# Stick-breaking weights by a running product on VectorE, with TensorE's side work in the second layer in a written order

## The chip, the cores and the metric

The kernel runs on one core of a Trainium2 chip. The metric is the device time of one execution in microseconds, lower is better. A core has five engines that run their own instruction streams in order and wait for each other by semaphores: TensorE (PE; its weight loads are shown apart as PEld), VectorE (DVE), ScalarE (ACT), GpSimd (POOL) and SyncE (SP), which here issues the DMAs.

## The reference, cut to what matters

One inference step of a decoder of two layers, for 256 prompt rows and 8 sample rows (264 columns in the kernel's layout) at model width 1024. Layer 0 mixes tokens by block-sparse softmax attention and a gated mixer, layer 1 by stick-breaking attention (8 heads of 64) and a causal pooling mixer with windows 2, 4, 8, 16. Each is followed by a convolutional FFN of width 2816. Norms, projections and residual adds stand around them. What changes is the stick-breaking attention:

```python
z = einsum('bqhd,bkhd->bhqk', q, k) * scale
before = kpos[None, :] < pos[:, None]
log_keep = where(before, log_sigmoid(-z), 0.0)
later = cumsum(log_keep, axis=3, reverse=True) - log_keep
w = where(before, exp(log_sigmoid(z) + later), 0.0)
out = einsum('bhqk,bkhd->bqhd', w, v)
```

The weight of key s for query t is sigmoid(z_ts) times the product of 1 - sigmoid(z_tj) over all keys j between s and t. The 256 prompt rows see each other; each sample row sees 256 cached keys, which lie in pages found through a page table.

## The kernel before

Activations lie transposed, features on the 128 partitions and 264 token columns in the free dimension. All weights stream from memory in the order of use, in blocks of 128x128. `run` walks through the blocks of a phase. For each it issues three matmuls (lines 329 to 331), since weights and activations are split into a high and a low half in fp32r: high by high, high by low, low by high. The split of a tile of eight blocks is one copy on ScalarE (`wh`, line 306) and one subtraction on VectorE (`wl`, line 307), three tiles ahead. The phases per layer are input projection (`in0`, `in1`), output projection (`out0`, `out1`), FFN gate and up (`ff`), and FFN down (`dn`). In layer 1 the input projection has 128 blocks: q and k (four tiles of eight blocks each, the four q tiles interleaved by half), then u (for the pooling), then v; the output projection has 64.

Everything else is side work hung into `run` at block counts, through `Hooks`: `hk.at(n, f)` calls f once 8(n+1) blocks are through. In which order an engine's instructions then stand is set by the framework's planner, which lays the program out by its own cost estimate; instructions wrapped in `keep_in_program_order` stay in the order in which they are written. Matmuls of the projections are not wrapped before the change, most side products neither. PSUM has two pools of four banks: `psm` ("mm") for the projections, `psa` ("at") for side work. 24 SBUF buffers of one size (`up`) are shared by activations, cache pages and work tiles.

Side work of the second layer, before the change:

- `nrm1.finish()`: squares of the residual rows are added on GpSimd (line 398) while the first layer's `dn` ends; a matmul with ones (`ns_n`, line 406) sums them over the partitions; Ln and Exp on ScalarE make the factor `R`, with which VectorE scales each projection result as it leaves PSUM (`in1_evac`).
- `zs_score`, `zs_soft`, `zs_cum`: scores of the samples against the cached keys (`sc`, line 451, 64 matmuls), turned over with the identity (line 921), softplus, sums over the keys by matmuls with a triangle of -1 (`negU`, lines 928 and 929), Exp.
- `z_qk(t)`, for a pair of heads: a matmul of identity by mask (line 882) sets the forbidden places to -1e30, then scores with keys on the partitions and queries in the free dimension (lines 884, 886); softplus by three ScalarE passes (Abs, Exp, Ln) and one VectorE operation (line 876).
- `z_cum(h)`, per head: the softplus is split into two fp32r halves (`Lh` on ScalarE, `Ll` on VectorE, lines 413, 414), matmuls with `negU` and with -1 (lines 900, 901) add for each key the sum over the later keys onto the scores in PSUM, and one Exp (line 902) gives the weights, keys on the partitions, as the value product needs them.
- `z_av(t)` (`av`, lines 494, 495): weights times values for a pair of heads; `sample_av` (line 465) and `sample_out` (line 478) the same for the samples. `v_pair` (line 489) transposes a tile of v.
- `pool_sum(t, o)`: per u tile about ten VectorE operations (lines 947 to 964), and `pool_mix(t)` a matmul (line 969).

The first layer's softmax attention (`s_qk`, `s_soft`, `s_tr`) has scores with queries on the partitions, and turns its weights over with three transposes per head (`pt`, line 684).

Of the kernel before, what the change touches and what calls it, by code (L numbers as in the profile page):

```python
# [18 lines left out]
P = 128  # L19
# [42 lines left out]
VL = 9  # L62
SQ = 4
SMO = -0.5
VL1 = 4
SQ1 = 4.5
ZQ0 = 5
ZQ1 = 1
ZC = 1
PM = 13  # L70
ZSS = 4.75
ZSC = 6
ZSA = 13
ZSO = 14.75
NA = 4
NB_ = 0.5
NEG = -1e30
# [143 lines left out]
@with_exitstack  # L221
def tile_decoder_step(ctx: ExitStack, tc: tile.TileContext, a):
    nc = tc.nc
    v, s, g, pe = nc.vector, nc.scalar, nc.gpsimd, nc.tensor
# [85 lines left out]
    def run(order, rhs, evac, hooks=None):  # L310
# [5 lines left out]
        for m, k in order:  # L316
# [15 lines left out]
            if left[m] == 0:  # L332
                evac(m, o)
            n += 1
            while hooks and n >= 8 * (hooks[0][0] + 1):
                for f in hooks.pop(0)[1]:
                    f()

# [23 lines left out]
    ident = cst("ident")  # L362
    ones = con.tile([P, P], F32, name="ones")
    v.memset(ones, 1.0)
    nones = con.tile([P, P], F32, name="nones")
    v.memset(nones, -1.0)
    epst = con.tile([P, 1], F32, name="epst")
    v.memset(epst, EPS)

# [113 lines left out]
    PZ = con.tile([P, NPG, NS, 32], F32, name="PZ")  # L483
    g.memset(PZ, 0.0)

    def v_pair(vt, src, t, name):
        p = at(f"vtp_{name}{t}")
        for kb in range(2):
            pe.transpose(p[:, kb * P:(kb + 1) * P], src[:, kb * P:(kb + 1) * P], ident)
        s.activation(vt[:, :, t * P:(t + 1) * P], p[:, :2 * P].rearrange("p (b d) -> p b d", b=2), AF.Copy)  # L490
# [5 lines left out]

    def gelu_set():
        tc.keep_in_program_order(s.preload_act_table_set("gelu_apprx_tanh_and_others"))

    def lnexp():  # L500
        tc.keep_in_program_order(s.preload_act_table_set("natural_log_exp_and_others"))
# [112 lines left out]
    maskb1 = con.tile([P, 384], BF16, name="maskb1")  # L614
    identb = con.tile([P, P], BF16, name="identb")

    def masks():
        tc.keep_in_program_order(v.tensor_copy(maskb0[:, 0:P], cst("m0")))
        v.tensor_copy(maskb0[:, SEQ:384], cst("m0"))
        v.tensor_copy(maskb1[:, 0:P], cst("m1"))  # L620
        v.tensor_copy(maskb1[:, SEQ:384], cst("m1"))
        for mk in (maskb0, maskb1):
            g.memset(mk[:, P:SEQ], 0.0)
        v.tensor_copy(identb, ident)

    q4, k4, v4 = f4("q4"), f4("k4"), f4("v4")
# [237 lines left out]
    icnt = cst("icnt").rearrange("p (g i) -> p g i", g=4)  # L864
    st1 = {}

    negU = con.tile([P, P], F32R, name="negU")
    v.tensor_copy(negU, cst("negU"))
    nonesr = con.tile([P, P], F32R, name="nonesr")
    v.tensor_copy(nonesr, nones)  # L870

    def softplus(e, z):
        s.activation(e, z, AF.Abs)
        s.activation(e, e, AF.Exp, scale=-1.0)
        s.activation(e, e, AF.Ln, bias=1.0)
        v.scalar_tensor_tensor(e, z, 0.0, e, ALU.max, ALU.add)

    def z_qk(t):
        pss = [at(f"Z1_{2 * t + i}") for i in range(2)]
        hd = [(q4[b:b + 64, t, :], k4[b:b + 64, t, :]) for b in (0, 64)]  # L880
        for ps in pss:
            pe.matmul(ps[:, :384], identb, maskb1, start=True, stop=False, skip_group_check=True)
        for ps, (qh, kh) in zip(pss, hd):
            tc.keep_in_program_order(pe.matmul(ps[:, 0:SEQ], kh[:, 0:P], qh[:, 0:SEQ], start=False, stop=False, skip_group_check=True))  # L884
        for ps, (qh, kh) in zip(pss, hd):
            tc.keep_in_program_order(pe.matmul(ps[:, SEQ:384], kh[:, P:SEQ], qh[:, P:SEQ], start=False, stop=False, skip_group_check=True))
        for i, ps in enumerate(pss):
            L = pp.tile([P, 384], F32, tag="p", name=f"L1_{2 * t + i}")
            softplus(L, ps[:, :384])
            st1["z", 2 * t + i] = (ps, L)  # L890

    def z_cum(h):
        ps, L = st1.pop(("z", h))
        if h % 2 == 0:
            st1["w", h // 2] = f4(f"w1_{h // 2}", (P, 2, 384))
        lh = pp.tile([P, 384], F32R, tag="ph", name=f"Lh_{h}", bufs=2)
        ll = pp.tile([P, 384], F32R, tag="pl", name=f"Ll_{h}", bufs=2)
        halves(lh, ll, L)
        for x in (lh, ll):
            pe.matmul(ps[:, 0:384], negU, x, start=False, stop=False, skip_group_check=True)  # L900
            pe.matmul(ps[:, P:SEQ], nonesr, x[:, SEQ:384], start=False, stop=x is ll, skip_group_check=True)
        s.activation(st1["w", h // 2][:, h % 2, :], ps[:, :384], AF.Exp)

    def z_av(t):
        w = st1.pop(("w", t))
        pav = at(f"pav1_{t}")
        for hh in range(2):
            av(pav, vt, w[:, hh, :], 2 * t + hh)
        halves(catA[0][:, t, :SEQ], catA[1][:, t, :SEQ], pav[:, :SEQ])

    def zs_score():
        ps = at("sc1")
        sample_score(ps, sample_q(q4, "l1"), ktiles, range(NS))
        z = st1["zs"] = pp.tile([P, PAST], F32, tag="p", name="zs")
        s.activation(z, ps[:, :PAST], AF.Copy)

    def zs_soft():
        z = st1["zs"]
        pc = at("pc")
        for pg in range(NPG):  # L920
            pe.matmul(pc[:, pg * P:(pg + 1) * P], z[:, pg * P:(pg + 1) * P], ident, start=pg == 0, stop=False, skip_group_check=True)
        L = pp.tile([P, PAST], F32, tag="p", name="L1s")
        softplus(L, pc[:, :PAST])
        st1["Ls"] = pc, L

    def zs_cum():
        pc, L = st1["Ls"]
        pe.matmul(pc[:, :PAST], cst("negU"), L, start=False, stop=False, skip_group_check=True)
        pe.matmul(pc[:, :P], nones, L[:, P:PAST], start=False, stop=True, skip_group_check=True)
        to_pz(pc, AF.Exp)  # L930
        st1["msk"] = f4("msk1", (P, 2, 512))

    def zs_out():
# [31 lines left out]
        st1["pl", t] = pl  # L965

    def pool_mix(t):
        pm = at(f"pm{t}")
        pe.matmul(pm[:, :T], pw[:, t, :], st1.pop(("pl", t)), start=True, stop=True)
        hh, ll = catB[0][:, t, :], catB[1][:, t, :]  # L970
        gs = vec("ps")[:, t:t + 1]
# [3 lines left out]
    def in1_evac(m, o):  # L975
# [11 lines left out]
    hk.at(SQ1, zs_score)  # L987
    for t in range(4):
        hk.at(ZQ0 + 2 * ZQ1 * t, z_qk, t)
        for h in (2 * t, 2 * t + 1):  # L990
            hk.at(ZQ0 + ZQ1 * h + ZC, z_cum, h)
    hk.at(8, lambda: nc.sync.dma_start(a["k1"], k4))
    for t in range(4):
        hk.at(PM - t, pool_mix, t)
    for t in range(3):
        hk.at(13 + t, lambda t=t: v_pair(vt, v4[:, t, :], t, "v1"))
    hk.at(14, z_av, 0)
    hk.at(15, z_av, 1)
    hk.at(15, z_av, 2)
    hk.at(ZSS, zs_soft)  # L1000
    hk.at(ZSC, zs_cum)
    hk.at(ZSA, sample_av_of(st1, PZ, vtiles, 0, "l1"))
    hk.at(ZSA + 1, sample_av_of(st1, PZ, vtiles, 1, "l1"))
    hk.at(ZSO, zs_out)
# [12 lines left out]
    _, nrm, evac = residual(vec("fin"), "fin", operand=False)  # L1017
# [71 lines left out]
```

## Time and profile before

| | us |
|---|---|
| runs: median of 3 (lowest to highest) | 618.79 (618.44 to 619.36) |
| profiled execution | 618.47 |
| its span | 616.4 |
| TensorE busy, share of the span | 97% |
| VectorE busy, share of the span | 67% |
| ScalarE busy, share of the span | 57% |

Granted TensorE clock over the span: 0.996 of full speed. The span runs from the first to the last instruction; about 2 us of an execution lie around it. Matmuls are pipelined, so the length of one (about 0.28 us) is more than its distance to the next (about 0.12); what one costs TensorE is read from starts. A start in the timeline is in microseconds from the span's start, followed by the length, and in brackets the engine's idle time before it and what ended that. In the rows by group, the numbers behind the bar are busy us, mean ns of one instruction, and idle time before. A window's row has its length, and then busy time and number of instructions of PE, PEld, DVE, ACT and POOL, the granted clock, the DMA share, and GB/s. In the chain of waits a row is start, length, and the work.

### The profile page before, as it was taken

To read this page: it belongs to the slowest core of one execution; us is meant where nothing else is said; L and a number is where in the kernel's file an instruction comes from. 1 tells how busy PE (TensorE), PEld (TensorE's weight loads), DVE (VectorE), ACT (ScalarE), POOL (GpSimd) and SP (SyncE) were. 2 spreads that over 40 slices of the span, in tenths; PEclk is the share of its full clock that TensorE was granted. 3 is DMA by queue.
4 is the path that set the end of the run, shared out by engine and by line. 5 is a ranking of instruction groups with operands and counts; after the bars stand their busy time and mean duration, and the time that the engine had idled before them with its cause. 6 is when DMAs were issued, how large, how long until landed. Compare 5 with 4: busy or idle time off the path is not lost.

```text
span 616.4 us, 12351 instructions
## 1 busy us (share of the span) xinstructions
PE 599.4 (97%) x4924; PEld 575.3 (93%) x4924; DVE 413.1 (67%) x704; ACT 350.4 (57%) x621; POOL 84.9 (14%) x111
## 2 busy tenths in 40 slices
PE   7899999999999999999999999999999999999994
PEld 5788987999999999999999997899999999999994
DVE  6986663969976676655555686396996766764441
ACT  5459763767756555644442757376765555554441
POOL 3330132324200000001110000042420000001020
PEclk9999999999999999999999999999999999999998
DMA  7995873543655445695477559944364555554502
GB/s 259 325 403 220 328 258 54 206 153 133 216 184 205 158 184 205 228 392 200 155 229 262 219 184 141 134 175 172 136 215 170 200 182 167 199 189 166 200 1 70
DMA packets 41354, 121.40 MB, mean 197 GB/s; under 512 B 17490, under 2 KB 19410, under 8 KB 29906
## 3 DMA queue, kind: packets, MB, share of 16 engines
q1 hardware_dynamic: 40178, 119.00, 59.3%
q10 hardware_dynamic: 1120, 1.63, 0.9%
q8 instruction: 38, 0.62, 0.4%
q14 instruction: 18, 0.15, 0.1%
HBM read 116.67 MB, written 3.94 MB: 196 GB/s over the span
## 4 chain that ended last, share of the span: by engine, by line
PE 84%; DVE 7%; issue 3%; DMA 2%; ACT 2%; POOL 1%; SPq 0%; DVEq 0%; ACTq 0%
PE mm L330 26%; PE mm L329 25%; PE mm L331 25%; DMA raw<-in_w 2%; DVE wl L307 2%; DVE xn_l L374 1%; PE pv_l L465 1%; PE sc L451 1%; PE pav L494 1%; PE Z L900 1%; DVE wk L542 1%; ACT wh L306 1%; PE Z L884 1%; POOL wk L553 0%; PE pt L684 0%
## 5 line engine op out<-in xcount | busy, mean ns | idle before, releaser
L307 DVE TENSOR_TENSOR wl<-raw,wh 128x1024 fp32r<-128x1024 f32 x183 | 229.4, 1255 | 129.1 <-ACT wh L306 129.0
L306 ACT ACTIVATE wh<-raw 128x1024 fp32r<-128x1024 f32 x183 | 193.7, 1059 | 182.5 <-PE mm L330 169.3
L330 PE MATMUL mm<-xn_l,wh 128*128 128x264 f32 x544 | 154.7, 284 | 1.7 <-DVE xn_l L374 1.5
L329 PE MATMUL mm<-xn_h,wh 128*128 128x264 f32 x544 | 153.8, 283 | 0.0
L331 PE MATMUL mm<-xn_h,wl 128*128 128x264 f32 x544 | 153.4, 283 | 0.0
L330 PEld LDWEIGHTS mm<-xn_l,wh 128*128 128x128 f32 x544 | 102.3, 188 | 2.5 <-DVE xn_l L374 2.5
L329 PEld LDWEIGHTS mm<-xn_h,wh 128*128 128x128 f32 x544 | 102.1, 188 | 0.0
L331 PEld LDWEIGHTS mm<-xn_h,wl 128*128 128x128 f32 x544 | 102.1, 188 | 0.0
L330 PE MATMUL mm<-a_l,wh 128*128 128x264 f32 x352 | 99.8, 284 | 0.0
L329 PE MATMUL mm<-a_h,wh 128*128 128x264 f32 x352 | 99.5, 284 | 0.0
L331 PE MATMUL mm<-a_h,wl 128*128 128x264 f32 x352 | 99.4, 283 | 0.0
L331 PEld LDWEIGHTS mm<-a_h,wl 128*128 128x128 f32 x352 | 66.2, 188 | 0.0
L330 PEld LDWEIGHTS mm<-a_l,wh 128*128 128x128 f32 x352 | 66.2, 188 | 0.0
L329 PEld LDWEIGHTS mm<-a_h,wh 128*128 128x128 f32 x352 | 66.0, 188 | 0.0
L329 PE MATMUL mm<-xg_h,wh 128*128 128x264 f32 x160 | 46.6, 298 | 3.6 <-DVE q L637 1.6
L330 PE MATMUL mm<-xg_l,wh 128*128 128x264 f32 x160 | 46.1, 293 | 0.0
L331 PE MATMUL mm<-xg_h,wl 128*128 128x264 f32 x160 | 44.7, 291 | 1.3 <-DVE wl L307 1.3
L329 PE MATMUL mm<-xg_f_h,wh 128*128 128x264 f32 x160 | 45.8, 286 | 0.0
L330 PE MATMUL mm<-xg_f_l,wh 128*128 128x264 f32 x160 | 45.4, 284 | 0.0
L331 PE MATMUL mm<-xg_f_h,wl 128*128 128x264 f32 x160 | 45.3, 283 | 0.0
L329 PE MATMUL mm<-xg_n_h,wh 128*128 128x264 f32 x128 | 37.4, 292 | 0.0
L331 PE MATMUL mm<-xg_n_h,wl 128*128 128x264 f32 x128 | 36.8, 288 | 0.0
(266 smaller groups left out, 1074.5 us busy)
## 6 DMA issues: line engine op xcount, KB each, us to landing
raw<-in_w SPq DMA_DIRECT2D x89, 1024.0 KB, 4.8
K<-in_kt SPq DMA_DIRECT2D x32, 256.0 KB, 6.0
V<-in_vp SPq DMA_DIRECT2D x32, 256.0 KB, 5.6
raw<-in_w SPq DMA_DIRECT2D x5, 512.0 KB, 5.3
CST<-in_cst SPq DMA_DIRECT2D x1, 548.0 KB, 5.5
XG<-in_x ACTq DMA_DIRECT2D x1, 528.0 KB, 7.8
out_k<-k SPq DMA_DIRECT2D x1, 528.0 KB, 9.4
out_v<-v SPq DMA_DIRECT2D x1, 528.0 KB, 3.0
```

The lines of the kernel that those rows point to most:

```text
L306: s.activation(h, src, AF.Copy)
L307: v.tensor_tensor(l, src, h.bitcast(F32), ALU.subtract)
L329: pe.matmul(o, h[:, c:c + P], xh, start=first, stop=False)
L330: pe.matmul(o, h[:, c:c + P], xl, start=False, stop=False)
L331: pe.matmul(o, l[:, c:c + P], xh, start=False, stop=left[m] == 0)
L374: j = v.scalar_tensor_tensor(l, src, gain, h.bitcast(F32), ALU.mult, ALU.subtract)
L451: pe.matmul(ps[32 * t:32 * t + 32, :PAST].rearrange("p (g k) -> p g k", g=NPG), qz[:, t, sq, :], kt[sq][:, :, t * P:(t + 1) * P], start=sq ...
L465: pe.matmul(pv[32 * j:32 * j + 32, :], pz[:, pg, sq, :], vtiles[sq][:, pg, :], start=pg == 0, stop=pg == NPG - 1)
L494: pe.matmul(o, vt[:, 0, h * HD:(h + 1) * HD], w[:, :SEQ], start=True, stop=False)
L542: v.scalar_tensor_tensor(C[:, 1:SEQ], G[:, 0:SEQ - 1], wc(1, j), C[:, 1:SEQ], ALU.mult, ALU.add)
L884: tc.keep_in_program_order(pe.matmul(ps[:, 0:SEQ], kh[:, 0:P], qh[:, 0:SEQ], start=False, stop=False, skip_group_check=True))
L900: pe.matmul(ps[:, 0:384], negU, x, start=False, stop=False, skip_group_check=True)
```

## The change

Three things change together.

First, the weights. Scores of the second layer now have queries on the partitions and keys in the free dimension, as in the first layer. ScalarE makes sigmoid(-z) and sigmoid(z) from PSUM; VectorE runs a product over the keys from the last to the first with `tensor_tensor_scan`, and one multiplication gives the weights (`stick`). The 384 columns hold the diagonal block of the first 128 queries and both blocks of the second 128; `edge`, with a single 1 in column 127, starts the product anew between the two parts, by the maximum with the second operand. `zs_soft`, `zs_cum`, `softplus`, `z_cum`, `negU` and `nones` fall away. The weights have to be turned over for the value product: three transposes per head (`z_tr`) and two for the samples (`zs_tr`). A table set with the sigmoid is loaded on ScalarE ahead of the stage, and the set with Ln and Exp behind the last `z_qk`.

Second, the mask matmuls of both layers write only the two diagonal blocks (256 columns by `two`), instead of 384 with zeros between.

Third, the order. `pe` is now an object whose `matmul` and `transpose` are wrapped in `keep_in_program_order` as long as `fixed[0]` is set, from just ahead of `in1` to the end of `out1`, so that all of TensorE's instructions written there, projections included, keep the order of the program. The side products get block counts of their own (`blk`), `pool_mix`, three `v_pair` and the samples' transposes get banks of the projections' pool (`mmb`), and all four `z_av` come behind block 8 of the output projection. V pages and the output of k1 stay at the block counts that they had.

```diff
-    add("negU", -(r[:, None] >= r[None, :]).astype(f))
-    add("m1", np.where(r[:, None] >= r[None, :], f(NEG), f(0)).astype(f))
+    add("m1", np.where(r[None, :] >= r[:, None], f(NEG), f(0)).astype(f))
...
+    class TensorE:
+        @staticmethod
+        def keep(i):
+            return tc.keep_in_program_order(i) if fixed[0] else i
+        def matmul(self, *x, **k):
+            return self.keep(nc.tensor.matmul(*x, **k))
+        def transpose(self, *x, **k):
+            return self.keep(nc.tensor.transpose(*x, **k))
...
+    def mmb(name):
+        return psm.tile([P, 512], F32, tag="mm", name=name)
...
+    def two(x):
+        return x.rearrange("p (b k) -> p b k", k=P)[:, 0:3:2, :]
...
-            pe.matmul(ps[:, :384], identb, maskb0, start=True, stop=False, skip_group_check=True)
+            pe.matmul(two(ps), identb, two(maskb0), start=True, stop=False, skip_group_check=True)
...
+    edge = f4("edge", (P, 384))
+    g.memset(edge, 0.0)
+    g.memset(edge[:, P - 1:P], 1.0)
+    def stick(w, z, n, e, name):
+        keep = pp.tile([P, n], F32, tag="keep", name=f"keep_{name}", bufs=2)
+        s.activation(keep, z, AF.Sigmoid, scale=-1.0)
+        s.activation(w, z, AF.Sigmoid)
+        v.tensor_tensor_scan(keep[:, ::-1], keep[:, ::-1], e[:, ::-1], 1.0, ALU.mult, ALU.max)
+        v.tensor_tensor(w[:, :n - 1], w[:, :n - 1], keep[:, 1:], ALU.mult)
...
-            tc.keep_in_program_order(pe.matmul(ps[:, 0:SEQ], kh[:, 0:P], qh[:, 0:SEQ], start=False, stop=False, skip_group_check=True))
+            pe.matmul(ps[:, 0:P], qh[:, 0:P], kh[:, 0:P], start=False, stop=False, skip_group_check=True)
         for ps, (qh, kh) in zip(pss, hd):
-            tc.keep_in_program_order(pe.matmul(ps[:, SEQ:384], kh[:, P:SEQ], qh[:, P:SEQ], start=False, stop=False, skip_group_check=True))
+            pe.matmul(ps[:, P:384], qh[:, P:SEQ], kh[:, 0:SEQ], start=False, stop=True, skip_group_check=True)
         for i, ps in enumerate(pss):
-            L = pp.tile([P, 384], F32, tag="p", name=f"L1_{2 * t + i}")
-            softplus(L, ps[:, :384])
+            w = st1["w", 2 * t + i] = pp.tile([P, 384], F32, tag="p", name=f"w1_{2 * t + i}")
+            stick(w, ps[:, :384], 384, edge, 2 * t + i)
+        if t == 3:
+            lnexp()
...
+    def z_tr(t):
+        pT = st1["pT", t] = f4(f"pT1_{t}", (P, 2, 384))
+        for hh in range(2):
+            w, pt = st1.pop(("w", 2 * t + hh)), at(f"pt1_{2 * t + hh}")
+            for i in range(3):
+                pe.transpose(pt[:, i * P:(i + 1) * P], w[:, i * P:(i + 1) * P], ident)
+            s.activation(pT[:, hh, :], pt[:, :384], AF.Copy)
...
+    sigmoid_set()
     hk = Hooks()
+    fixed[0] = True
+    blk = lambda b, f, *x: hk.at(b / 8 - 1, f, *x)
     for n in range(8):
-        hk.at(VL1 + n, drip_of(vload, 2))
...
+        blk(40 + 8 * n, drip_of(vload, 2))
+    blk(48, zs_score)
+    blk(58, zs_tr)
+    for t, b in enumerate((52, 66, 80, 94)):
+        blk(b, z_qk, t)
+    for t, b in enumerate((62, 76, 90, 104)):
+        blk(b, z_tr, t)
+    blk(72, lambda: nc.sync.dma_start(a["k1"], k4))
+    for i, b in enumerate((92, 100, 108, 116)):
+        blk(b, pool_mix, 3 - i)
+    for t, b in enumerate((112, 120, 127)):
+        blk(b, lambda t=t: v_pair(vt, v4[:, t, :], t, "v1", mmb))
+    for i, b in enumerate((116, 122)):
+        blk(b, sample_av_of(st1, PZ, vtiles, i, "l1"))
+    blk(126, zs_out)
     run(orders["in1"], pick(xg), in1_evac, hk)
     nc.sync.dma_start(a["v1"], v4)
     hk = Hooks()
-    hk.at(-0.5, lambda: v_pair(vt, v4[:, 3, :], 3, "v1"))
-    hk.at(0, z_av, 3)
+    blk(6, lambda: v_pair(vt, v4[:, 3, :], 3, "v1"))
+    for t in range(4):
+        blk(8, z_av, t)
...
     run(orders["out1"], pick([catA, catB]), evac, hk)
+    fixed[0] = False
     R = nrm.finish()
```

More of the change, by code (lines that the diff above doesn't have):

```diff
@@ L223, in tile_decoder_step @@
     nc = tc.nc
-    v, s, g, pe = nc.vector, nc.scalar, nc.gpsimd, nc.tensor
+    v, s, g = nc.vector, nc.scalar, nc.gpsimd
+    fixed = [False]
+    class TensorE:
[6 more added lines that the diff above has]
+            return self.keep(nc.tensor.transpose(*x, **k))
+    pe = TensorE()
     con = ctx.enter_context(tc.tile_pool(name="con", bufs=1))
@@ L334, in run @@
             n += 1
-            while hooks and n >= 8 * (hooks[0][0] + 1):
+            while hooks and n >= round(8 * (hooks[0][0] + 1)):
                 for f in hooks.pop(0)[1]:
@@ L484, in tile_decoder_step, with v_pair @@
     g.memset(PZ, 0.0)
-    def v_pair(vt, src, t, name):
-        p = at(f"vtp_{name}{t}")
+    def v_pair(vt, src, t, name, bank=None):
+        p = (bank or at)(f"vtp_{name}{t}")
         for kb in range(2):
@@ L865, in tile_decoder_step @@
     st1 = {}
[L867 to L876, printed above, removed]
+    edge = f4("edge", (P, 384))
[7 more added lines that the diff above has]
+        v.tensor_tensor(w[:, :n - 1], w[:, :n - 1], keep[:, 1:], ALU.mult)
     def z_qk(t):
@@ L881, in z_qk @@
         for ps in pss:
-            pe.matmul(ps[:, :384], identb, maskb1, start=True, stop=False, skip_group_check=True)
+            pe.matmul(two(ps), identb, two(maskb1), start=True, stop=False, skip_group_check=True)
         for ps, (qh, kh) in zip(pss, hd):
-            tc.keep_in_program_order(pe.matmul(ps[:, 0:SEQ], kh[:, 0:P], qh[:, 0:SEQ], start=False, stop=False, skip_group_check=True))
+            pe.matmul(ps[:, 0:P], qh[:, 0:P], kh[:, 0:P], start=False, stop=False, skip_group_check=True)
@@ L885, in z_qk @@
         for ps, (qh, kh) in zip(pss, hd):
-            tc.keep_in_program_order(pe.matmul(ps[:, SEQ:384], kh[:, P:SEQ], qh[:, P:SEQ], start=False, stop=False, skip_group_check=True))
+            pe.matmul(ps[:, P:384], qh[:, P:SEQ], kh[:, 0:SEQ], start=False, stop=True, skip_group_check=True)
         for i, ps in enumerate(pss):
-            L = pp.tile([P, 384], F32, tag="p", name=f"L1_{2 * t + i}")
-            softplus(L, ps[:, :384])
[L890 to L902, printed above, removed]
+            w = st1["w", 2 * t + i] = pp.tile([P, 384], F32, tag="p", name=f"w1_{2 * t + i}")
@@ L906, in z_av @@
-        pav = at(f"pav1_{t}")
+        pav, pT = at(f"pav1_{t}"), st1.pop(("pT", t))
         for hh in range(2):
-            av(pav, vt, w[:, hh, :], 2 * t + hh)
+            av(pav, vt, pT[:, hh, :], 2 * t + hh)
         halves(catA[0][:, t, :SEQ], catA[1][:, t, :SEQ], pav[:, :SEQ])
@@ L913, in zs_score, with zs_tr @@
         sample_score(ps, sample_q(q4, "l1"), ktiles, range(NS))
[L914 to L919, printed above, removed]
-        for pg in range(NPG):
[L921 to L930, printed above, removed]
+        w = st1["zs"] = pp.tile([P, PAST], F32, tag="p", name="zs")
+        stick(w, ps[:, :PAST], PAST, edge[:, P:], "s")
+    def zs_tr():
+        pP = mmb("pP1")
+        for pg in range(NPG):
+            pe.transpose(pP[:, pg * P:(pg + 1) * P], st1["zs"][:, pg * P:(pg + 1) * P], ident)
+        to_pz(pP, AF.Copy)
         st1["msk"] = f4("msk1", (P, 2, 512))
@@ L967, in pool_mix @@
     def pool_mix(t):
-        pm = at(f"pm{t}")
+        pm = mmb(f"pm{t}")
         pe.matmul(pm[:, :T], pw[:, t, :], st1.pop(("pl", t)), start=True, stop=True)
```

35 lines of the change are left out of this document (2 added, 33 removed).

## The prediction

> **What bounds the kernel now.** I read the page's busy shares first, then the chain of work that ended last, then the windows of the stage that is changed.
>
> ```profile
> PE 599.4 (97%) x4924; PEld 575.3 (93%) x4924; DVE 413.1 (67%) x704; ACT 350.4 (57%) x621; POOL 84.9 (14%) x111
> PE 84%; DVE 7%; issue 3%; DMA 2%; ACT 2%; POOL 1%; SPq 0%; DVEq 0%; ACTq 0%
> 315.50:414.20 98.70, 98.61 (x814) 88.35 (x812) 62.28 (x121) 55.50 (x104) 9.17 (x24) 1.00 0.82 187
> 350.00:360.00 10.00, 10.00 (x73) 8.63 (x71) 9.22 (x23) 6.22 (x13) 0.67 (x8) 1.00 0.66 254
> ```
>
> The first two lines are shares of the whole span: TensorE is busy for 97% of it and carries 84% of the chain. The third is a window: second layer's input and output projections (from the first matmul on `xg_n` to the first of the second FFN), with busy time of PE, PEld, DVE, ACT and POOL. TensorE has no hole in it, so whatever TensorE no longer does there shortens the kernel, as long as nobody keeps it waiting. The fourth warns of that: for ten of these microseconds VectorE is busy 9.22, where the pooling sums meet the attention.
>
> **The yardstick.** Projection matmuls follow each other at 0.121 us (starts 315.25, 315.37, 315.50 below), three to a block, so a block of weights takes 0.363 us. The stage has 128 + 64 blocks, 576 matmuls, 69.7 us; the other 98.6 - 69.7 = 28.9 us go to side products and to waiting between them.
>
> **What the side products will cost.** From the chain of waits in order of time (start, length, work), and one passage of TensorE's timeline:
>
> ```profile
> 53.06 0.65 PE pt L684 x6
> 335.76 3.59 PE sc L451 x64
> 350.29 0.18 PE Z L882
> 350.47 0.63 PE Z L884 x4
> 351.11 0.22 PE Z L886 x4
> 358.48 0.63 PE Z L884 x2
> 365.67 0.44 PE pm L969 x2
> 381.62 1.85 PE pv_l L465 x16
> 392.35 0.22 PE vtp_v L489 x2
> 384.07 0.59 PE pav L494 x4
> 384.66 0.22 PE pav L495 x4
> 100.41 0.87 PE po_l L478 x8
> 352.55 0.28 PE L329 MATMUL mm<-xg_n_h,wh 128*128 128x264 f32 x1
> 352.67 0.34 PE L900 MATMUL Z<-Lh,negU 128*128 128x384 f32 x1
> 352.85 0.22 PE L901 MATMUL Z<-Lh,nonesr 128*128 128x128 f32 x1
> 352.91 0.33 PE L330 MATMUL mm<-xg_n_l,wh 128*128 128x264 f32 x1
> ```
>
> Removed: per head two pairs of summing matmuls (L900, L901). A pair widens the gap between projection matmuls from 0.12 to 0.36 us, about 0.26 with the slower next start; 16 pairs are 4.2 us. The samples' own sums (L928, L929) and the matmuls with the identity ahead of them (L921) go too; two single transposes come in their place. They need no price here, since the new list is priced whole below.
>
> Added: `z_tr`, six transposes per pair of heads, the same work as first layer's L684: 0.65 us a pair, 2.6 us for four.
>
> Cut: the mask matmul streams 256 columns for 384, 0.18 to 0.12 us; 16 of them in both layers, half a microsecond in each.
>
> Fixed order: before, the planner put other work between the two heads of a pair, and each then paid by itself the 0.63 us (358.48 is one of them) that two heads together pay once (350.47). That, and holes of some tenths before the late summing matmuls, go as well.
>
> It is safer to price the new list than the difference. Scores of samples 3.8; four `z_qk` at 1.30 (two masks 0.24, 0.85 for the rest, 0.2 to get in and out); two plus 24 transposes 0.25 + 2.64; four pool mixes 1.8; four V transposes 0.9; two sample products 3.9; their transposes 0.95; four value products 3.45; the norm's sum 0.45: 23.4 us. Against 28.9 this is -5.5 us, and the first layer's masks give -0.5.
>
> **Wait one: the norm's sum at the head of the stage.** The changed program's order, engine by engine, has one move that the diff does not spell out. The sum over partitions for the second layer's norm (`ns_n`, L406) stood behind 14 blocks of the input projection. Every projection matmul is now kept in program order, and the program writes the norm first: so it stands directly behind the last FFN matmul, ahead of every projection. TensorE must wait there for what these rows show:
>
> ```profile
> 315.25 0.28 PE L330 MATMUL mm<-a_l,wh 128*128 128x264 f32 x1
> 315.37 0.28 PE L331 MATMUL mm<-a_h,wl 128*128 128x264 f32 x1
> 315.50 0.28 PE L329 MATMUL mm<-xg_n_h,wh 128*128 128x264 f32 x1
> 315.63 1.06 ACT L306 ACTIVATE wh<-raw 128x1024 fp32r<-128x1024 f32 x1 [1.84 <-PE mm L330]
> 315.69 0.43 DVE L572 TENSOR_TENSOR XG<-XG,mm 128x264 f32<-128x264 f32 x1 [0.65 <-PE mm L331]
> 316.60 0.50 ACT L373 ACTIVATE xg_n_h<-XG,VEC 128x264 fp32r<-128x264 f32 x1
> 317.00 0.41 ACT L386 ACTIVATE sq_n<-XG 128x264 f32<-128x264 f32 x1
> 317.55 1.01 POOL L398 TENSOR_TENSOR acc_n<-acc_n,sq_n 128x264 f32<-128x264 f32 x1 [7.66 <-ACT sq_n L386]
> ```
>
> Residual add, weight split, operand, square, add on GpSimd: the engines' orders here are unchanged but for two small memsets ahead of the add, which wait for a buffer released some microseconds earlier. The add ends at 318.56, so the sum starts at about 318.65 where a projection matmul started at 315.50: +3.15 us. Nothing covers it, because all that could is queued behind it. The split's look-ahead does not suffer: four tiles (32 blocks) are ready when it ends.
>
> **Wait two: third pair of heads.** Ready times in us from the stage's first projection matmul, TensorE unheld. `z_qk` of heads 2, 3 ends at 31.3 (66 blocks, 24.0, and 7.3 of side products). The transposes of heads 4, 5 are due at block 90: 32.7 + 9.3 = 42.0, end 42.6. VectorE's durations:
>
> ```profile
> L876 DVE SCALAR_TENSOR_TENSOR L<-Z,L 128x384 f32<-128x384 f32 x8 | 4.2, 552 | 2.6 <-ACT L L875 2.6
> L873 ACT ACTIVATE L<-Z 128x384 f32<-128x384 f32 x8 | 3.5, 487 | 4.3 <-PE Z L886 4.2
> 349.73 1.23 DVE L307 TENSOR_TENSOR wl<-raw,wh 128x1024 fp32r<-128x1024 f32 x1 [0.65 <-ACT wh L306]
> 350.87 0.55 DVE L414 TENSOR_TENSOR Ll<-L,Lh 128x384 fp32r<-128x384 f32 x1
> 351.34 0.42 DVE L947 TENSOR_TENSOR pool<-mm,R_n 128x256 f32<-128x256 f32 x1
> 351.67 0.16 DVE L948 TENSOR_TENSOR PALL<-mm,R_n 128x8 f32<-128x8 f32 x1
> ```
>
> By starts, a weight split takes 1.14, a 384-wide operation 0.47, a 256-wide one 0.33, a small one about 0.13. No row shows a scan. Below it costs no less than the 384-wide L876 (0.55 long). Above, I bound it by a second pass over its elements: the slope between L947 (256, 0.42) and L307 (1024, 1.23) is 1.05 ns an element, 0.40 for 384, so 0.95. I take the upper end, since each element needs the one before it, which no row's operation does. Then scan, product, scan, product of heads 2, 3 (first sigmoid 0.49 after 31.3) end at 34.9. In the listed order VectorE then has eleven 256-wide operations of the pooling sums (3.7), nine small (1.2), two splits (2.3), and scans and products of heads 4, 5 (2.8): 10.0, to 44.9. TensorE's last three transposes (0.33) end at 45.2, not 42.6: +2.6. With the cheap scan it comes to +1.1.
> [...]
>
> The other three pairs, in the same way: heads 0, 1 due 28.2, ready 28.0; heads 2, 3 due 35.25, ready 35.0; heads 6, 7 due 52.7, ready 52.6 (both later by wait two). No wait, but margins of 0.1 to 0.2.
>
> **What lies beside other work.** ScalarE does three passes per head for five, and gains two table loads, one behind the norm and one behind the last sigmoid; it is busy for 55.5 of the stage's 98.7 us, and its weight splits run tiles ahead of their use. V pages and `out_k1` are issued at the same block counts; V's buffers are free before their issue, and last is needed at block 122, over 10 us later. The constants shrink by one 128x128 matrix, loaded long before this stage. Pool mixes and V transposes move to the projections' PSUM banks; the bank each needs is read out a block or more earlier. If any cover is gone, the price is the wait itself, since TensorE is in order.
>
> **Sum.** -5.5 - 0.5 + 3.15 + 2.6 = -0.25. The profiled execution took 618.47 us (616.4 span and 2.1 around it); the median of the runs is 618.79, 0.3 above it. I predict 618.3: no measurable change, a change being measurable from about 0.2%, 1.2 us.
>
> **The rivals.**
> *Cheap scan.* If it costs like L876, wait two is 1.1 and the sum -1.75: 616.7. For it: the row with the same operand sizes. Against it: the dependence.
> *The clock halves during wait one.* Rows of the kernel's end (windows, with the granted clock third from the right) and of its start:
>
> ```profile
> 608.39 0.71 PE L406 MATMUL ns_fin<-sq_fin,ones 128*128 128x264 f32 x2 [0.59 <-ACT sq_fin L386]
> 611.00:611.20 0.20, 0.00 (x0) 0.00 (x0) 0.20 (x2) 0.00 (x0) 0.00 (x0) 1.00 0.00 0
> 611.40:611.60 0.20, 0.00 (x0) 0.00 (x0) 0.20 (x1) 0.00 (x0) 0.00 (x0) 0.50 0.81 285
> 1.47 3.59 PE L357 MATMUL warm<-warm 128*128 128x512 bf16 x8 [1.47 <-DVE warm L354]
> 6.11 0.42 PE L331 MATMUL mm<-xg_h,wl 128*128 128x264 f32 x1
> 6.33 0.42 PE L329 MATMUL mm<-xg_h,wh 128*128 128x264 f32 x1
> ```
>
> The last matmul ends at 609.10 and the clock is at half from 611.3 on, 2.2 us later; in wait one TensorE stands still for 3.0 us (315.65 to 318.65). After an idle start, matmuls still ran at 0.22 us for 0.12 at 6.33, five us behind the first. So a fall costs half of some 3 to 5 us, 1.5 to 2.5: 619.8 to 620.8, slower. It decides if a drop needs under 3 us without matmuls. Against it: at the end TensorE had idled already before its last matmul (the 0.59 in its row), so the 2.2 us understate what is needed.
> [...]
> *The margins go.* If scans or sigmoids are a few tenths later, three more transposes wait 0.3 to 0.7 each: 619.2 to 620.4. For it: 9.22 of 10 us busy on VectorE already.
> *The saving is larger than listed*, for instance wait two vanishing because VectorE finishes the pooling sums sooner: 615.7 at best, since wait one stays.
>
> **How the numbers follow.** As forecast 0.38; cheap scan 0.21; clock 0.18; margins 0.15; larger saving 0.08. Faster (below 617.55 by the median): a fifth of the first, four fifths of the second, all of the last: 0.33. Slower (above 620.0): two thirds of the clock case, half of the margins, a little of the first: 0.22. Same: the rest, 0.45. The forecast's own range is 617.3 to 619.3; from 616.2 to 620.8 less than 2 in 10 is left out.
>
> **What would show it.** Wait one: a hole of 3 us on TensorE ended by POOL's `acc_n`, with the `ns_n` matmul right behind. Wait two: TensorE idle before `pt` of heads 4, 5, ended by a VectorE product (L890). The scan: its mean, 0.55 or 0.95. The side products: busy count and gaps of the stage, its from the first FFN's last matmul to the second FFN's first 98.7 us before and 99.0 expected. I am wrong if wait one is not there, if the scan costs twice the upper bound, or if the clock column leaves 1.00 in mid-kernel.

## The result, and the profile after

| | us | against the kernel before, measured beside it (95% interval) |
|---|---|---|
| before: median of 5 runs | 618.44 | |
| after: median of 5 runs (lowest to highest) | 621.20 (620.75 to 621.86) | 1.0043 (1.0028 to 1.0058) |
| after: profiled execution, its span | 620.75, 618.9 | span before 616.4 |

The change makes the kernel 0.43% slower. No change was forecast, at 618.3, and 621.2 lies above the stated range, which ended at 620.8.

The page of the changed kernel, with the busy shares and the chain of work that ended last:

```profile
PE 595.6 (96%) x4910; PEld 573.6 (93%) x4910; DVE 418.1 (68%) x702; ACT 345.9 (56%) x605; POOL 85.8 (14%) x111
PE 82%; DVE 7%; issue 4%; ACT 3%; DMA 2%; POOL 1%; SPq 0%; DVEq 0%; ACTq 0%; POOLq 0%
```

TensorE does less (595.6 us for 599.4) in a longer span: it now waits, or runs slowly. The windows of the changed kernel show where. The first row is the whole stage, the others are the passage behind its head (granted clock third from the right):

```profile
315.63:415.74 100.11, 95.01 (x800) 86.12 (x798) 67.39 (x123) 51.57 (x88) 9.82 (x24) 0.98 0.77 188
319.20:319.40 0.20, 0.20 (x3) 0.17 (x2) 0.00 (x0) 0.00 (x0) 0.20 (x1) 1.00 0.92 246
319.40:319.60 0.20, 0.20 (x4) 0.20 (x3) 0.00 (x0) 0.12 (x1) 0.20 (x3) 0.63 0.80 297
320.00:322.00 2.00, 2.00 (x11) 2.00 (x11) 0.00 (x0) 1.70 (x2) 0.00 (x0) 0.50 0.76 315
322.80:323.00 0.20, 0.20 (x3) 0.20 (x2) 0.00 (x0) 0.00 (x0) 0.00 (x0) 0.83 0.21 82
```

The stage takes 100.1 us for 98.7, and TensorE stands still for 5.1 us of it, where before it had no hole. The clock falls to half at 319.45 (0.63 over 0.2 us is 0.05 us at full speed) and comes back at 322.87.

Wait one, from the timeline of the changed kernel:

```profile
315.51 0.28 PE L223 MATMUL mm<-a_h,wl 128*128 128x264 f32 x1
317.62 1.06 POOL L404 TENSOR_TENSOR acc_n<-acc_n,sq_n 128x264 f32<-128x264 f32 x1 [7.07 <-ACT sq_n L392]
318.73 0.71 PE L223 MATMUL ns_n<-acc_n,ones 128*128 128x264 f32 x2 [2.94 <-POOL acc_n L404]
319.09 0.48 PE L223 MATMUL mm<-xg_n_h,wh 128*128 128x264 f32 x1
319.79 0.42 PE L223 MATMUL mm<-xg_n_h,wh 128*128 128x264 f32 x1
320.01 0.42 PE L223 MATMUL mm<-xg_n_l,wh 128*128 128x264 f32 x1
```

A hole of 2.94 us, ended by GpSimd's last addition, with the norm's sum right behind. Then projection matmuls follow each other at 0.22 us (319.79, 320.01) until the clock is back: 3.41 us at half speed.

Wait two, TensorE's timeline of the changed kernel, and VectorE's in the same stretch:

```profile
362.67 0.28 PE L223 MATMUL mm<-xg_n_h,wl 128*128 128x264 f32 x1
364.75 0.52 PE L226 MATMUL pt<-CST,w 128*128 128x128 f32 x3 [1.80 <-DVE w L890]
365.62 0.52 PE L226 MATMUL pt<-CST,w 128*128 128x128 f32 x3 [0.35 <-DVE w L890]
365.90 0.37 PE L223 MATMUL mm<-xg_n_h,wh 128*128 128x264 f32 x1
```

```profile
360.39 1.22 DVE L315 TENSOR_TENSOR wl<-raw,wh 128x1024 fp32r<-128x1024 f32 x1
361.52 0.42 DVE L955 TENSOR_TENSOR pool<-pool 128x256 f32<-128x256 f32 x1
361.94 0.95 DVE L889 TENSOR_TENSOR_SCAN keep<-keep,edge 128x384 f32<-128x384 f32 x1
362.87 0.95 DVE L889 TENSOR_TENSOR_SCAN keep<-keep,edge 128x384 f32<-128x384 f32 x1
364.06 0.55 DVE L890 TENSOR_TENSOR w<-w,keep 128x383 f32<-128x383 f32 x1
364.93 0.55 DVE L890 TENSOR_TENSOR w<-w,keep 128x383 f32<-128x383 f32 x1
```

The gap between projection matmuls is 365.90 - 362.67 - 0.12 = 3.11 us. A pair of heads that does not wait takes 0.58 here (348.56 to 349.26 in the same trace, less 0.12), so the wait costs 2.53. VectorE is busy without a break: a weight split, the two running products, the two multiplications (L890), and pooling sums between them.

### The profile page after: what moved, and what is told of

It is laid out like the page before. It is cut to its first block, busy times and chain, and to the rows that moved or that the text cites. A ratio compares the mean times of both kernels' runs of the same rounds, so it can differ in the third digit from the quotient of the medians.

```text
span 618.9 us, 12324 instructions
## 1 busy us (share of the span) xinstructions
PE 595.6 (96%) x4910; PEld 573.6 (93%) x4910; DVE 418.1 (68%) x702; ACT 345.9 (56%) x605; POOL 85.8 (14%) x111
## 4 chain that ended last, share of the span: by engine, by line
PE 82%; DVE 7%; issue 4%; ACT 3%; DMA 2%; POOL 1%; SPq 0%; DVEq 0%; ACTq 0%; POOLq 0%
PE mm L223 76%; DVE wl L315 2%; DMA raw<-in_w 2%; DVE xn_l L380 1%; PE sc L223 1%; PE pv_l L223 1%; ACT wh L314 1%; PE pav L223 1%; PE pt L226 1%; DVE wk L551 1%; PE Z L223 1%; POOL wk L562 0%; PE S L223 0%; DVE wk L547 0%; DVE wk L552 0%
## 5 line engine op out<-in xcount | busy, mean ns | idle before, releaser
L223 PE MATMUL mm<-xg_n_h,wh 128*128 128x264 f32 x128 | 39.3, 307 | 0.0
L223 PE MATMUL mm<-xg_n_l,wh 128*128 128x264 f32 x128 | 37.1, 290 | 0.0
```

The lines of the kernel that those rows point to most:

```text
L223: return self.keep(nc.tensor.matmul(*x, **k))
```

## The experiments

**The norm's sum put back behind 14 blocks.**

```diff
-    xg, R = xg1, nrm1.finish()
+    xg = xg1
...
-    sigmoid_set()
...
+    def norm1():
+        nonlocal R
+        R = nrm1.finish()
+        sigmoid_set()
+
+    blk(14, norm1)
```

> The norm's sum of the second layer stands behind 14 blocks of the input projection again, as in the kernel before; everything else is as in the changed kernel. Theory (the hole of 2.9 us at the head of the stage costs 3.2 us, and the half clock behind it, 17 projection matmuls at 0.22 for 0.12 us, another 1.8): 5.0 us less than the changed kernel, 616.2 us, and the clock column stays at 1.00 there. Rival (the clock falls there for another reason than the hole): only 3.2 us less, 618.0, with the half clock still to be seen. Rival (the norm is merely late elsewhere, its reciprocal root holding up the first evacuation): less than 3 us gained, with a hole on TensorE around block 20.

Measured: 616.50 us, 0.9968 of the kernel before (0.9956 to 0.9981), 4.6 us less than the changed kernel by the ratios. Its stage, from the windows:

```profile
316.05:411.44 95.39, 93.24 (x800) 84.52 (x798) 67.25 (x123) 51.66 (x88) 9.84 (x24) 1.00 0.80 197
```

95.39 us for 100.11, clock at 1.00, and the 2.15 us without TensorE that are left are wait two. The place of the norm's sum (the sigmoid's table load moves with it) cost 4.7 us of the stage. What share of it is the clock's, this run can't say.

**TensorE kept busy in the wait.**

```diff
     for i, x in enumerate(parts):
+    # ahead of the second layer's sum only, 14 times:
+    tc.keep_in_program_order(pe.matmul(p, warm[:, :P], warm, start=True, stop=True))
```

> The changed kernel with 14 matmuls on the constant of the warm-up, 512 columns each, issued between the last FFN matmul and the norm's sum: the wait stays as long as it was, but TensorE is not idle in it. Theory (the idle hole halves the clock, and that costs 1.8 us): projection matmuls follow at 0.12 from the first on, 619.4 us, 1.8 less than the changed kernel. Rival (the half clock comes from something else, such as the sum in 32-bit itself or its releaser): matmuls behind the sum still at 0.22, 621.2 us.

Measured: 620.02 us, ratio 1.0018 (1.0001 to 1.0034). Timeline and window behind the sum:

```profile
316.72 3.20 PE L223 MATMUL ns_n<-warm 128*128 128x512 bf16 x14
319.82 0.71 PE L223 MATMUL ns_n<-acc_n,ones 128*128 128x264 f32 x2
```

```profile
320.20:323.00 2.80, 2.80 (x24) 2.77 (x23) 0.00 (x0) 2.19 (x3) 0.60 (x4) 1.00 1.02 347
```

The sum starts as late as before (3.22 us behind the last FFN matmul, 316.60, in both), but 24 matmuls pass in 2.8 us at full clock, and the stage takes 98.56 us. So 1.55 us of the 4.7 (100.11 - 98.56) were the halved clock. Nothing but the filling of TensorE's idle time was changed; that the idleness was the cause rests here on this one profiled execution.

**The transposes of heads 4 to 7 later.**

```diff
-    for t, b in enumerate((62, 76, 90, 104)):
+    for t, b in enumerate((62, 76, 98, 110)):
```

> The changed kernel with the transposes of heads 4 and 5 at block 98 for 90 and those of heads 6 and 7 at block 110 for 104. Theory (wait two is TensorE standing before a product that VectorE finishes 2.5 us late): 2.5 us less, 618.7 us, with no hole before these transposes. Rival (VectorE is behind for the whole passage, so the wait goes to the next pair, or to a pool mix): at most 1 us less, 620.2 to 621.2, with a hole before the transposes of heads 6 and 7 or a pool mix.

Measured: 618.23 us, ratio 0.9988 (0.9977 to 1.0000), 3.4 us less than the changed kernel by the ratios and so more than the 2.5 expected. The wait did not go elsewhere: each pair of transposes takes 0.57 or 0.58 us. The rest is a surprise in the profiled execution, whose hole at the head is the same:

```profile
316.19 0.28 PE L223 MATMUL mm<-a_h,wl 128*128 128x264 f32 x1
319.41 0.71 PE L223 MATMUL ns_n<-acc_n,ones 128*128 128x264 f32 x2 [2.94 <-POOL acc_n L404]
319.76 0.48 PE L223 MATMUL mm<-xg_n_h,wh 128*128 128x264 f32 x1
320.08 0.28 PE L223 MATMUL mm<-xg_n_l,wh 128*128 128x264 f32 x1
```

The clock stayed at 1.00 (in the windows 319.50 to 321.00 and 321.10 to 322.00), behind a hole of the same 2.94 us. Its stage is 96.16 us: 2.4 less for wait two and 1.55 less for the clock.

**Both.**

> Both: the norm's sum behind 14 blocks and the two pairs of transposes later. Theory (the three losses are separate and add): 5.0 + 2.5 = 7.5 us less than the changed kernel, 613.7 us, about 4.7 less than the kernel before. Rival (with wait one gone VectorE loses the time that the wait gave it to run ahead, so new waits come up in front of transposes or pool mixes): 614.5 to 616 us.

Measured: 614.33 us, ratio 0.9927 (0.9913 to 0.9941). The stage:

```profile
315.46:408.44 92.98, 92.98 (x800) 84.65 (x798) 66.81 (x123) 51.15 (x88) 10.25 (x24) 1.00 0.82 202
```

No hole is left. The losses are separate and add: 100.1 - 93.0 = 7.1 us. With nothing waiting, the stage shows the price of the side products alone: 92.98 - 69.7 = 23.3 us.

**The norm's sum at the head, in the kernel before.**

```diff
-            pe.matmul(p[:, :T], ones, x, ...)
+            mm = pe.matmul(p[:, :T], ones, x, ...)
+            if name == "n1":
+                tc.keep_in_program_order(mm)
...
+            keep = tc.keep_in_program_order if order is orders["in1"] and n < 32 else lambda x: x
```

(`keep` is then put around the three projection matmuls.)

> The kernel before with one thing of the change: the norm's sum of the second layer is held at the head of the stage, ahead of the first 32 blocks of its input projection. Theory: the hole costs 3.2 us wherever the sum stands at the head, so 618.6 + 3.2 = 621.8 us in executions whose clock stays up and 1.6 more, 623.4, where it is halved behind the hole. Which of the two it is hangs on how much of the hole lies in one stretch of the 3.413 us grid on which the granted clock has changed so far (2.69 us idle in one stretch: halved; 1.80: not). Rival (the planner makes up for it, by other work in the hole): under 1 us, 618.6 to 619.6.

Measured: 623.27 us (single runs from 620.66 to 625.76), ratio 1.0067 (1.0042 to 1.0092). The hole is again 2.94 us, here from 315.56 to 318.50, and the clock is lower for longer:

```profile
317.40:317.60 0.20, 0.00 (x0) 0.00 (x0) 0.20 (x1) 0.00 (x0) 0.15 (x1) 1.00 1.55 135
317.60:317.80 0.20, 0.00 (x0) 0.00 (x0) 0.20 (x2) 0.00 (x0) 0.20 (x1) 0.55 1.55 136
319.00:324.00 5.00, 5.00 (x23) 4.80 (x22) 0.00 (x0) 0.91 (x2) 0.48 (x4) 0.50 0.67 242
```

It fell at 317.62 and was back at 324.45, 6.83 us later, which is two times 3.41. So wait one needs nothing else of the change.

**The running product replaced by a cheaper operation.**

```diff
-        v.tensor_tensor_scan(keep[:, ::-1], keep[:, ::-1], e[:, ::-1], 1.0, ALU.mult, ALU.max)
+        v.tensor_tensor(keep, keep, e, ALU.max)
```

> The changed kernel with each running product replaced by an element-wise maximum of the same size with the edge constant, so that the running product is left out of the computation. Theory (VectorE's queue carries wait two, and a running product costs 0.4 us more than an element-wise operation): four of them stand ahead of the product that TensorE waits for, so the hole before the transposes of heads 4 and 5 shrinks from 2.5 us to about 1.0, and the time by 1.5, to 619.7 us where the clock is halved and 618.1 where not. Rival (the hole is set by the releases from ScalarE or by the pooling sums alone): 2.5 us of hole as before.

Measured: 618.80 us, ratio 0.9998 (0.9983 to 1.0014). The operation took 552 ns for 952 (groups below), and the gap at the transposes of heads 4 and 5 fell from 3.11 to 1.66, a wait of 1.08 us. The prediction's arithmetic had 1.1 for this price. The profiled stage takes 98.65 us, 1.46 less than the changed kernel's, as the wait says; the ratios differ by 2.8 us, and the rest of that no run explains. The clock was halved here too, 0.50 in the window 318.60 to 321.80.

```profile
L889 DVE TENSOR_TENSOR keep<-keep,edge 128x384 f32<-128x384 f32 x8 | 4.4, 552 | 2.7 <-ACT keep L887 2.6
```

**The new weights with the planner's order.**

```diff
-    fixed[0] = True
+    fixed[0] = False
```

> The new weights without the fixed order: the order of the side products is left to the planner, with the same block positions as its wishes. In its list the norm's sum stands behind 14 blocks and the transposes of heads 4 and 5 at block 96.7. Theory (the new weights gain some 5.5 us and the fixed order lost it): no hole at the head, a stage of 93 to 94 us, 614 to 615 us. Rival (the planner's list splits pairs and leaves holes of its own): a stage of 95 to 97 us, 616 to 618 us.

Measured: 614.44 us, ratio 0.9935 (0.9916 to 0.9953), stage 94.20 us. All of the change but the fixed order is worth 4 us; the fixed order, as written, gave back all of that and 2.7 more. With the two places mended, the fixed order's stage is 1.2 us shorter than the planner's (92.98). Over the whole kernel the two can't be told apart: 0.9927 and 0.9935, with intervals that overlap.

**The first layer.** Its narrower masks should have saved half a microsecond, and no saving shows. The timeline of VectorE in the changed kernel has a weight split (40.20) ahead of the first row maximum (41.88), where before the row maximum stood first (40.15) and the split behind it (40.68). The mask matmul of head 4 (the first of the third pair, and called the third mask in the expectations) then waits for the exponentials that hang on these maxima; rows of the changed kernel:

```profile
40.20 1.76 DVE L315 TENSOR_TENSOR wl<-raw,wh 128x1024 fp32r<-128x1024 f32 x1
41.88 0.28 DVE L679 TENSOR_REDUCE st<-S 128x1 f32<-128x128 f32 x1
43.49 0.27 PE L223 MATMUL S<-maskb,identb 128*128 128x256 bf16 x1 [1.11 <-ACT p L683]
```

Tested by narrow masks in the first layer of the kernel before, and nothing else:

```diff
-            pe.matmul(ps[:, :384], identb, maskb0, start=True, ...)
+            pe.matmul(two(ps), identb, two(maskb0), start=True, ...)
```

> The kernel before with the narrow mask matmul in the first layer alone. VectorE's listed order there is the swapped one, a weight split ahead of head 0's row maximum. Theory (the swap costs 0.4 to 1.4 us at the third mask, the eight narrow matmuls save 0.5): a hole of 0.8 to 1.9 us between projection matmuls at the third mask for 0.46 in the kernel before, and a time of -0.1 to +0.9 us, 618.5 to 619.5 us. Rival (the hole in the changed kernel belongs to something else in it): hole of 0.46, 0.5 us less, 618.1 us.

Measured: 618.77 us, ratio 0.9999 (0.9991 to 1.0008), and the swap with its hole is there:

```profile
39.61 1.75 DVE L307 TENSOR_TENSOR wl<-raw,wh 128x1024 fp32r<-128x1024 f32 x1
41.28 0.28 DVE L671 TENSOR_REDUCE st<-S 128x1 f32<-128x128 f32 x1
42.89 0.27 PE L661 MATMUL S<-maskb,identb 128*128 128x256 bf16 x1 [0.87 <-ACT p L675]
```

The gap between projection matmuls at this mask is 1.06 us, for 0.46 before. The interval of the ratio is -0.6 to +0.5 us: nothing saved on the median, though the forecast's half microsecond lies just inside it. And the other way round, on top of the version with both repairs, with the full-width mask for the first layer's heads 0 to 3:

```diff
+            if t <= 1:
+                pe.matmul(ps[:, :384], identb, maskb0, start=True, ...)
+            else:
                 pe.matmul(two(ps), identb, two(maskb0), start=True, ...)
```

> As the one with the norm behind 14 blocks and the later transposes, with the full-width mask matmul for the first layer's heads 0 to 3, which puts VectorE's row maximum of head 0 ahead of a weight split again. Theory (the narrow masks saved 0.5 us in the first layer and the swapped VectorE order lost 0.6 to 1.4 at the third mask): the hole of 0.85 to 1.9 us at the third mask falls to 0.5, half the saving stays, 0.3 to 0.8 us less, 613.5 to 614.0. Rival (that hole is set by ScalarE's table or the exponentials, not by the swap): hole as before, 614.5 us.

Measured: 613.00 us, ratio 0.9909 (0.9891 to 0.9927), the lowest median, 5.6 us below the kernel before; its interval overlaps that of both repairs alone (0.9913 to 0.9941). The row maximum is first again, and the mask matmul of head 4 leaves a gap of 41.36 - 40.66 - 0.12 = 0.58 us, for 0.85 with both repairs alone:

```profile
39.73 0.27 DVE L683 TENSOR_REDUCE st<-S 128x1 f32<-128x128 f32 x1
40.26 1.23 DVE L315 TENSOR_TENSOR wl<-raw,wh 128x1024 fp32r<-128x1024 f32 x1
```

```profile
40.66 0.28 PE L223 MATMUL mm<-xg_h,wh 128*128 128x264 f32 x1
41.34 0.27 PE L223 MATMUL S<-maskb,identb 128*128 128x256 bf16 x1 [0.39 <-ACT p L687]
41.36 0.37 PE L223 MATMUL mm<-xg_l,wh 128*128 128x264 f32 x1
```

In all four profiles whose rows stand here this mask starts 1.6 us behind the first row maximum (41.75 - 40.15 before, 43.49 - 41.88 after, 42.89 - 41.28 and 41.34 - 39.73 in the two tests), so the row maximum sets its time. The gap that it leaves varies from execution to execution, though: 0.85 to 1.88 us in the ten profiles with the split first, and 0.46, 0.58 and 1.01 us in the three with the row maximum first. The difference is about half a microsecond on the average, and the two overlap.

**The clock, twice more.** With 7 of the filling matmuls instead of 14, and the changed kernel itself once more:

> The changed kernel with 7 of the warm-up's matmuls ahead of the norm's sum, so that TensorE's hole there is 1.5 us for 2.9; the sum starts no sooner. Theory (a stretch of the 3.413 us grid with 2.06 us or more idle halved the clock and one with 1.80 did not): no stretch can hold 1.8, so the clock stays up in every execution, 1.0 to 1.6 us under the changed kernel run beside it on the average, 619.5 to 620.2 us, and 1.00 in the clock column behind the sum. Rival (any hole at the head is enough, or the sum itself): as the changed kernel beside it, 621.2 us, at half clock.

> The changed kernel once more, beside the others. Theory (the grid's position is new in every execution, the hole of 2.94 us holds the critical 1.8 to 2.06 us in one stretch for 66 to 81% of the positions): 621.2 us on the median with single executions from about 619.5, and in the profiled one half clock behind the norm's sum if 2.06 us or more of the hole lies in one stretch, full clock if under 1.8. Rival (the clock falls behind every such hole): half clock whatever the position.

Measured, in the same order: 619.32 us, ratio 1.0025 (1.0007 to 1.0043), and 622.10 us, ratio 1.0052 (1.0036 to 1.0068). First the hole and the clock of the one with 7, then the clock of the repetition, whose hole again ends at 318.73:

```profile
318.18 0.71 PE L223 MATMUL ns_n<-acc_n,ones 128*128 128x264 f32 x2 [1.41 <-POOL acc_n L404]
```

```profile
318.60:322.00 3.40, 3.40 (x29) 3.37 (x28) 0.00 (x0) 2.48 (x4) 0.56 (x4) 1.00 1.04 367
```

```profile
319.20:320.00 0.80, 0.80 (x8) 0.77 (x7) 0.00 (x0) 0.48 (x2) 0.51 (x4) 1.00 1.47 384
320.20:323.40 3.20, 3.20 (x16) 3.20 (x16) 0.00 (x0) 1.50 (x2) 0.00 (x0) 0.50 0.69 289
```

A hole of 1.41 us left the clock at 1.00. In the repetition the clock fell only at 320.10, over a microsecond after TensorE had begun to work again. Of the 12 runs with 7 filling matmuls, five lie at 621.3 to 624.6 and seven at 618.3 to 619.4. Only one execution has a profile, at full clock. The mean granted clock is on record for all: 0.987 to 0.993 in the long ones, 0.993 to 0.995 in the others. So the clock was lower in the long ones on the average, but where in the kernel it fell is not recorded; "in every execution" is not shown, and for those five the rival isn't excluded.

## Why the prediction was wrong

| term, us | predicted | measured |
|---|---|---|
| side products of the stage | -5.5 | -5.6 (28.9 before, 23.3 without waits) |
| wait one | +3.15 | +3.2 |
| wait two | +2.6 | +2.5 |
| half clock behind wait one | 0 (rival, 0.18) | +1.55 |
| first layer | -0.5 | +0.1 |
| behind the stage | 0 | +1.0 |

The measured terms add to 2.75, and the spans differ by 2.5; the four terms of the stage are 0.25 more than its 1.40 together. The first layer's +0.1 is one execution against one: in the nine profiles with the changed kernel's first layer the stage begins between 314.7 and 316.7 us.

*The step that failed is the rejection of the clock rival.* It said that the kernel's end, 2.2 us of standing still behind the last matmul and then half clock, understated what is needed, since TensorE had idled already before that matmul. The conclusion drawn was that more than a 3 us hole might be needed. Counted out, the same rows gave the answer: in the 3.41 us before that fall (607.88 to 611.29), TensorE was idle for 0.51 and 2.19 us, 2.7 together. A hole of 2.94 us holds as much, if it lies right; in the changed kernel 2.69 of it lay in one stretch. The place, the price range (1.5 to 2.5) and the cause of the rival were right; its chance was not. The price was half of "some 3 to 5 us" at half clock: the 5 is read from a row, the 3 was the author's estimate and no row shows it; the runs had 3.41, and 6.83 in one. The fall came in four of the five profiled executions with the whole hole, and with it the sign of being wrong that the prediction had named, a clock column that leaves 1.00 in mid-kernel. It is the largest part of the miss: 1.55 of the 2.75 us between the forecast sum, -0.25, and the spans' +2.5.

The falls and rises of the clock in one execution are multiples of 3.413 us apart. In the changed kernel, windows of 0.2 us put them at 8.84, 12.25, 319.45, 322.87 and 613.00; from the first to the last 604.16 us pass, 177 steps of 3.413. This grid lies elsewhere in another execution of the same kernel: in the repetition, with the hole at the same place, the clock fell at 320.10. That its position is new in every execution, as the expectation for the repetition took it, was the author's assumption: in three rows of the last section's table the grid has a bound at 317.60 to 317.62. Nor was a whole idle stretch of the grid needed for a fall: in the changed kernel 2.69 us of one did it.

*The first layer's half microsecond* did not show either. The swap of one split with one row maximum on VectorE was passed over. That the swap eats the saving is likely and not shown: its effect on the gap at one mask is the size of the saving on the average, but that gap differs by more between executions of one order.

*Behind the stage* 1.0 us more passes, which no step foresaw: the last FFN takes 0.3 us longer (193.4 us from its first matmul to the first of the last norm's sum, for 193.1), and from there to the end 9.85 us pass for 9.21. The FFN's 0.3 is in all ten profiles of kernels with the new weights and in none of the three with the old. Between the kernel before and the changed one it builds up in steps of about 0.04 us, spread over the phase. The end varies more, 9.4 to 9.85 against 9.2; up to the last issue of an output transfer both kernels take 5.6 us, and all of the difference lies in the waits behind that. The cause of both stays open.

*Right:* the list of the side products (23.4 predicted, 23.3 measured), the move of the norm's sum and its releaser, the third pair of heads, and the running product at 0.95 us. The thin margins of the other three pairs held: 0.58 us each, no wait. The cheap-scan rival fell with the running product's price, but its arithmetic stood (1.1 predicted, 1.08 measured with the cheaper operation).

## What to carry to other kernels

Writing an engine's order by hand writes its waits too. Go through the list with the time at which each instruction's input is ready, and put every one that is not ready behind work that is; here two such places cost 7.1 us, more than the new algorithm gained. A hole on TensorE can cost twice, as the wait and as half clock behind it: here 3.2 us and 1.55, and the least idle time in one stretch that lost the clock was 1.65 us. Where it cannot be moved, filling matmuls in it can save the second: with 14 of them the profiled stage took 98.56 us for 100.11. When an edit makes an engine's instruction shorter, compare the planned order of the other engines too.

## What the runs showed of the hardware

The clock went by how much of one stretch of the 3.413 us grid TensorE stood idle, and not by the length of the hole alone: behind holes of the same 2.94 us it was halved with 2.05 to 2.78 us in one stretch, and stayed up with 1.80. Here are all profiled executions with a hole at the head of the stage; the stretch is the one that holds most of the hole, placed by that execution's own falls and rises:

| execution | hole | stretch | idle in it | clock after it |
|---|---|---|---|---|
| replaced running product | 314.90 to 317.84 | 315.06 to 318.47 | 2.78 | half |
| changed kernel | 315.79 to 318.73 | 316.04 to 319.45 | 2.69 | half |
| sum at the head of the kernel before | 315.56 to 318.50 | 314.20 to 317.62 | 2.06 | half |
| changed kernel again | 315.79 to 318.73 | 316.69 to 320.10 | 2.05 | half |
| later transposes | 316.47 to 319.41 | 317.61 to 321.02 | 1.80 | full |
| 7 filling matmuls | 316.77 to 318.18 | 314.19 to 317.60 | 0.84 | full |

By these rows alone the bound would lie between 1.80 and 2.05 us idle of 3.41. The beginning of one kernel shows that it isn't so sharp. In the version with both repairs the clock fell at 8.66 us (0.66 below), and TensorE had been idle for only 1.65 us of the stretch from 5.25 on; wait two of the version with 14 filling matmuls, 1.80 us within one stretch (361.11 to 364.53), left it at full. Timeline and window of the one, timeline of the other:

```profile
8.43 0.36 PE L223 MATMUL mm<-xg_h,wh 128*128 128x264 f32 x1 [1.65 <-DVE wh L311]
8.60:8.80 0.20, 0.20 (x3) 0.20 (x2) 0.20 (x1) 0.20 (x2) 0.00 (x0) 0.66 1.20 494
364.30 0.52 PE L226 MATMUL pt<-CST,w 128*128 128x128 f32 x3 [1.80 <-DVE w L893]
```

In the stretches named here, counted between the modelled ends of matmuls, 0.84 us idle kept the clock, 1.65 lost it at the beginning of a kernel, 1.80 kept it twice, and 1.99 (changed kernel, TensorE idle from 6.81 to 8.80 ahead of its fall at 8.84) and more lost it. What else counts between 1.65 and 1.99 stays open.

To get the clock back took, in the executions named here, a stretch without idle time: in the third row the next stretch (317.62 to 321.03) had 0.88 us idle and stayed at half, and only the full one behind it (321.03 to 324.45) ended it. The stretches that ended it in the changed kernel (8.84 to 12.25 and 319.45 to 322.87) had no idle time either. So the same hole of 2.94 us cost one stretch at half clock in three executions, two in a fourth and none in a fifth.

The running product costs 2.0 ns per element by its slope, where an element-wise operation costs 1.05 by that of the prediction's rows; group rows of the changed kernel:

```profile
L889 DVE TENSOR_TENSOR_SCAN keep<-keep,edge 128x384 f32<-128x384 f32 x8 | 7.6, 952 | 2.5 <-ACT keep L887 2.3
L889 DVE TENSOR_TENSOR_SCAN keep_s<-keep_s,edge 128x256 f32<-128x256 f32 x1 | 0.7, 694 | 1.8 <-ACT keep_s L887 1.8
```

(952 - 694) / 128 = 2.0 ns, 1.9 times the 1.05.
